# First rows of a hybrid SSD and MLP layer: shift and scale of tiles 1 to 5 singly, products high by high first

## The chip, the core and the metric

The kernel runs on one core of a Trainium2 chip. The metric is the time of one execution on the device, in microseconds (us). TensorE, VectorE (DVE), ScalarE (ACT), GpSimd (POOL) and the DMA queue of SyncE (SP) are the engines that appear in the rows; PEld is TensorE's weight load, which overlaps its products.

## The reference

The layer takes 256 latent tokens x and 256 context tokens ctx of width 2048, normalises each row, scales and shifts it by values that a vector c (for ctx: c_ctx) gives through a matrix w_ada, and projects the result with w_in. Cut to what the change touches:

```python
shift, scale, gate = jnp.split(silu(c) @ w_ada + b_ada, 3, axis=-1)
shift_c, scale_c, gate_c = jnp.split(silu(c_ctx) @ w_ada + b_ada, 3, axis=-1)
hc = _rmsnorm(ctx, g_pre) * (1.0 + scale_c) + shift_c
hx = _rmsnorm(x, g_pre) * (1.0 + scale[:, None]) + shift[:, None]
zc = hc @ w_in[:, :XBC_W + DT_W]
zx = hx @ w_in
```

What follows (convolution, a scan in both directions, a gated MLP, two norms, the output projection and the residual with gate) is the same before and after.

## The kernel before, in words

The model width is cut into 16 tiles (KT) of 128 rows. The token axis has 512 columns: the context half CTX is columns 0 to 255, the latent half 256 to 511. x stands transposed in `xT`.

All large products are done in three: a value is split into a high part (rounded to fp32r) and a low part (the rest), and high by high, high by low and low by high are added up in PSUM (`mm3`, lines 141 to 143). For the normalised rows the parts are `hhi` and `hlo`, for the weights `hi_st` and `lo_st`.

The **first rows** are the stage before the large weight stream. It makes `hhi` and `hlo` for all 16 tiles and, as each tile is ready, adds its share to the dt product (`psdt`, 512 columns, two products a tile: lines 418) and to seven output tiles psx0 to psx6. psx3 and psx6 have only the 256 latent columns. So a tile's products are 17 of 512 columns and 6 of 256.

Shift and scale of a tile need a product of silu(c) and silu(c_ctx) (`sc`, 32 columns, two used) with two megabytes of w_ada, the ada loads 2n and 2n+1. They run on 32-column groups of TensorE, four side by side. There are three forms:
- tile 0: `ada_mm` (line 249), 64 products of 64 columns, each of four column groups holding 32 of the tile's rows; `ada_fin` (line 257) transposes the result from PSUM on DVE, and two ACT operations (lines 262, 264) make `ha` (scale) and `hb` (shift);
- tiles 1 to 3: `ada_rows` (line 219), 16 products of 256 columns, each column group holding a quarter of the sum; `ada_keep` (224) copies that to SBUF, `ada_sum` (230) adds the four groups up and turns them with two products, `ada_one` (235, 237) makes `ha` and `hb` from PSUM;
- tiles 4 to 15 in pairs: `ada_mm` with 128 columns for two tiles at once, four ada loads, then `ada_fin` and `ada_ab`.

`make_h` (lines 365, 368, 370) then multiplies both halves of x by scale and 1/rms (`rb`) on DVE, adds the shift on ACT (that is `hhi`) and makes `hlo` on DVE. `split_hi` (ACT, line 352), `split_dt` (DVE, 356) and `split_lo` (DVE, 360) split the weights, `wst`.

The order on TensorE, DVE, ACT and POOL is written out by hand. For each tile kt, `row_steps(kt)` gives a list: ("m", -1) to ("m", 6) are the products dt and psx0 to psx6 of tile kt, the other letters prepare tile n = kt + 1. `STEPS` names their functions. SP's loads are issued in program order: for each kt the ada loads 2kt+6 and 2kt+7 and the weights of tile kt+2. ada loads have six buffers, weights three, the parts of the weights three. `warm` issues products with no use while the kernel waits for its first data.

After the first rows the weights w_xbc, w_lat and w_out stream through in pieces of 1 MB.

Of the kernel before, what the change touches and what calls it, by code (L numbers as in the profile page):

```python
# [8 lines left out]
F32 = mybir.dt.float32  # L9
F32R = mybir.dt.float32r  # L10
BF16 = mybir.dt.bfloat16
AF = mybir.ActivationFunctionType
ALU = mybir.AluOpType
PSUM = bass.MemoryType.PSUM

P = 128
D = 2048
# [8 lines left out]
WST = 64 + NST * P  # L26

WH = 64 + 3 * P
NSING = 4

LAST = (-1, 4, 5, 0, 1, 2, 3, 6)

# [12 lines left out]
def tile_hybrid_ssd_mlp(  # L45
# [126 lines left out]
    def spt(shape, name):  # L172
        return sps.tile(shape, F32, tag="s", name=name)
# [33 lines left out]

    ada_ps = {}

    def ada_rows(c):  # L210

        u, k0 = c // 2, 8 * (c % 2)
        if k0 == 0:
            ada_ps[u] = spt([P, 512], f"psada{u}")
        ps = ada_ps[u]
        raw = ada_raw.pop(c)
        for kk in range(8):
            g = kk % 4
            nc.tensor.matmul(ps[32 * g : 32 * g + 32, 0:256], lhsT=sc[:, k0 + kk, :], rhs=raw[:, kk * 256 : (kk + 1) * 256],
                             start=k0 == 0 and kk < 4, stop=k0 > 0 and kk >= 4)  # L220

    def ada_keep(u):
        cp = st2.tile([P, 256], F32, tag="cp", name=f"adac{u}")
        nc.vector.tensor_copy(cp, ada_ps[u][:, 0:256])
        ada_ps[u] = cp, ada_ps[u][:, 256:260]

    def ada_sum(u):
        cp, pt = ada_ps[u]
        for q in range(2):
            nc.tensor.matmul(pt[:, 2 * q : 2 * q + 2], lhsT=cp[:, q * P : (q + 1) * P], rhs=sel[:, 0, 0:2],  # L230
                             start=True, stop=True)

    def ada_one(u):
        pt = ada_ps.pop(u)[1]
        nc.scalar.activation(ha[:, u, :], pt[:, 0:2], AF.Identity, bias=bsc1[:, u : u + 1],
                             scale=pc[:, C_GPRE + u : C_GPRE + u + 1])
        nc.scalar.activation(hb[:, u, :], pt[:, 2:4], AF.Identity, bias=pc[:, C_BADA + u : C_BADA + u + 1])

    def ada_mm(ci):
        u, n, k0, nk = ada_place(ci)  # L240
        if k0 == 0:
# [10 lines left out]
    def ada_fin(u):  # L252

        ps = ada_ps.pop(u)
        n = 64 * len(UNITS[u])
        ada_ps[u] = tr = st2.tile([P, 128], F32, tag="row", name=f"adat{u}")
        nc.vector.transpose(tr[:, 0:n], ps[:, 0:n])
        ada_ab(u, 0)

    def ada_ab(u, q):  # L260
        kt, tr = UNITS[u][q], ada_ps[u]
        nc.scalar.activation(ha[:, kt, :], tr[:, 64 * q : 64 * q + 2], AF.Identity, bias=bsc1[:, kt : kt + 1],
                             scale=pc[:, C_GPRE + kt : C_GPRE + kt + 1])
        nc.scalar.activation(hb[:, kt, :], tr[:, 64 * q + 32 : 64 * q + 34], AF.Identity,
                             bias=pc[:, C_BADA + kt : C_BADA + kt + 1])
# [6 lines left out]

    def wst_load(kt):
        w = st3.tile([P, WST], F32, tag="wst", name=f"wst{kt}")
        nc.sync.dma_start(w, wst[kt])
        wraw[kt] = w

    for t in range(4):
# [24 lines left out]
    def warm(*ns):  # L303
        for n in ns:
            nc.tensor.matmul(psw[:, 0:n], lhsT=ones, rhs=ones[:, 0:1].to_broadcast([P, n]), start=True, stop=True)
# [25 lines left out]
    nc.vector.reciprocal(rc, rc)  # L331
    nc.vector.tensor_copy(ss4.rearrange("p (b i) -> p b i", i=32), bc(rc, 2, 32))
    nc.vector.transpose(rb, ss4)
    ada_mm(0)
    ada_mm(1)
    warm(512, 512)
    psdt = spt([P, TOK], "psdt")
    psx = []
    for i in range(6):
# [18 lines left out]
    def split_lo(kt, a=64, b=WST):  # L358
        hi, lo = sp0[kt]
        nc.vector.tensor_tensor(lo[:, a - 64 : b - 64], wraw[kt][:, a:b], hi[:, 64 + a : 64 + b].bitcast(F32), op=ALU.subtract)  # L360

    def make_h(kt):
        sl = (slice(256, 512), slice(0, 256))
# [17 lines left out]
    def row_steps(kt):  # L381


        m = [("m", i) for i in range(-1, NST)]
        if kt == KT - 1:
            out_ = [("m", i) for i in LAST]
            out_.insert(3, ("t", 0))
            for i in range(2):
                out_.insert(out_.index(("m", 4 + i)) + 1, ("z", i))
            return out_  # L390
        n = kt + 1
        s_ = [("c", n), ("d", n), ("l", n)]

        a = [("a", c) for c in range(2 * kt + 2, min(2 * kt + 6, 2 * KT))] if n >= NSING and kt % 2 else []
        f = [("f", (n - NSING) // 2 + NSING)] if kt % 2 else []
        f2 = [("f2", (n - NSING) // 2 + NSING)] if kt % 2 else []
        c_, d_, l_, h_ = s_ + [("h", n)]
        if n < NSING:
            r = [("r", 2 * n), ("r", 2 * n + 1)]
            g = m[4:5] + [("g", n), ("o", n), h_]  # L400
            if n < 3:
                q = 5 - n
                return m[:q] + r + [c_, ("k", n), d_, ("l1", n)] + g + [("l2", n)] + m[q:4] + m[5:]
            return m[:3] + r + s_ + [("k", n)] + g + m[3:4] + m[5:]
        if n == NSING:
            return m[:2] + a[:2] + m[2:3] + a[2:] + [c_] + f + [d_, ("l1", n), h_, ("l2", n)] + f2 + m[3:]
        if n == NSING + 1:
            return m[:3] + [h_] + s_ + m[3:]
        if n == NSING + 2:
            return m[:2] + a + s_ + f + [h_] + f2 + m[2:]  # L410
        return s_ + a + f + [h_] + f2 + m

    STEPS = {"a": ada_mm, "f": ada_fin, "f2": lambda u: ada_ab(u, 1), "r": ada_rows, "k": ada_keep, "g": ada_sum, "o": ada_one,
             "h": make_h, "c": split_hi, "d": split_dt, "l": split_lo,
             "l1": lambda n: split_lo(n, 64, WH), "l2": lambda n: split_lo(n, WH)}

    def dt_mm(kt, low):
# [26 lines left out]
    split_hi(0, 0, WH)  # L444
    ada_fin(0)
    split_dt(0)
    make_h(0)
    split_lo(0, 64, WH)
    split_hi(0, WH)
    split_lo(0, WH)  # L450
    for kt in range(KT):
# [810 lines left out]
def _layout(i):  # L1262
    import numpy as np

    i = {k: np.asarray(v) for k, v in i.items()}
    x, c, cx = i["x"][0], i["c"][0], i["ctx"][0]
    w_in, w_out, w_ada = i["w_in"][0], i["w_out"][0], i["w_ada"][0]
    order = _tile_order()
    a = {}
    xc = np.concatenate([cx, x], axis=0)  # L1270
    a["xch"] = xc.T.reshape(4, 4, P, TOK).transpose(0, 2, 1, 3).reshape(4, P, D)
    a["xtok"] = x.reshape(2, P, D)
    a["ccols"] = np.stack([c.reshape(KT, P).T, i["c_ctx"].reshape(KT, P).T], axis=2)
    wada = np.empty((48, P, D), w_ada.dtype)
    ss = w_ada[:, : 2 * D].reshape(KT, P, 2, KT, 4, 32)[:, :, ::-1].transpose(0, 1, 4, 3, 2, 5)
    for kt in range(NSING):
        r = ss[:, :, :, kt] if kt == 0 else ss[:, :, :, kt].transpose(0, 1, 3, 2, 4)
        wada[2 * kt : 2 * kt + 2] = r.reshape(2, 8, P, 256).transpose(0, 2, 1, 3).reshape(2, P, D)
    for m in range(NSING, KT, 2):
        wada[2 * m : 2 * m + 4] = ss[:, :, :, m : m + 2].reshape(4, 4, P, 512).transpose(0, 2, 1, 3).reshape(4, P, D)  # L1280
    wada[32:] = w_ada[:, 2 * D :].reshape(KT, P, 16, P).transpose(2, 3, 0, 1).reshape(16, P, D)
    a["wada"] = wada
    cw = i["conv_w"][0].reshape(5, 32, P)[:, order].transpose(2, 1, 0).reshape(P, 160)
    cb = i["conv_b"][0].reshape(32, P)[order].T
    a["pcols"] = np.concatenate(
        [i["b_ada"][0].reshape(48, P).T, i["g_pre"][0].reshape(KT, P).T, i["g_ssd"][0].reshape(KT, P).T,
         i["g_mlp"][0].reshape(KT, P).T, i["b_s"][0].T, cw, cb], axis=1)
    a["dtp"] = np.stack([i["dt_bias"][0].reshape(64), i["a_log"][0].reshape(64)])
    a["dskip"] = i["d_skip"].reshape(1, 32)
    a["gpost"] = i["g_post"].reshape(1, D)  # L1290
    a["gv"] = i["g_v"].reshape(1, D)
    a["crow"] = c.reshape(1, D)
    wk = w_in.reshape(KT, P, -1)
    xbc = wk[:, :, :4096].reshape(KT, P, 32, P)[:, :, order]
    a["wst"] = np.concatenate([wk[:, :, 4096:4160], xbc[:, :, list(FIRST)].reshape(KT, P, NST * P)], axis=2)
    a["wxbc"] = xbc[:, :, list(REST)].transpose(2, 1, 0, 3).reshape(len(REST), P, D)
    cols = {"z": 4160, "u": 6208, "v": 8256, "m": 10304}
    blocks = []
    for n in "vumz":
# [29 lines left out]
```

## Time and profile before

| | us |
|---|---|
| median of 3 runs | 989.73 |
| lowest and highest run | 989.63, 991.26 |
| span of the profiled execution, first to last instruction | 987.9 |
| TensorE busy in the span | 978.8 |
| DVE busy | 621.4 |
| ACT busy | 495.4 |

A row of the timeline has the start in us, the duration in us (for a row that merges several instructions, from the first's start to the last's end), the engine, the line of the kernel, the operation, output <- inputs, the tile's shape and, in brackets, the idle time of the engine just before it with what ended it. Records of consecutive products overlap, so the distance of two starts is what a product costs, and not its duration. On TensorE each fp32 product stands as two records, each fp32r product as one.

### The profile page before, as it was taken

What the parts mean: (1) busy time and instruction counts of PE and PEld (TensorE: products, weight loads), DVE (VectorE), ACT (ScalarE), POOL (GpSimd) and SP (SyncE); (2) the same over time, 40 slices, a digit from 0 to 9 for tenths busy, and PEclk for the clock granted to TensorE, in tenths of its full rate; (3) what the DMA queues carried; (4) which work ended last, traced back from release to release, by engine and by line L of the source; (5) the groups of instructions that cost most, each with busy time, mean ns of one, the idle gap of its engine ahead of it and who ended that gap; (6) DMA issues with size and microseconds to landing.
All of it is one profiled execution on the core that took longest, in us unless ns stands there. A gap on an engine that the chain in (4) does not pass through costs nothing.

```text
span 987.9 us, 13929 instructions
## 1 busy us (share of the span) xinstructions
PE 978.8 (99%) x5502; PEld 792.6 (80%) x5502; DVE 621.4 (63%) x949; ACT 495.4 (50%) x762; POOL 112.5 (11%) x162
## 2 busy tenths in 40 slices
PE   9999999999999999999999999999999999999997
PEld 4688888778887878787888888887888888888885
DVE  4444488868886566756767766767555564445636
ACT  4233358566665554545445343454565563346522
POOL 0000002432453222224000000000000000000000
PEclk9999999999999999999999999999999999999999
DMA  9999844233323424145877768774455446556722
GB/s 372 421 418 418 352 149 166 86 129 128 128 75 139 142 98 145 43 169 206 297 302 284 275 257 296 280 274 170 170 180 203 171 170 213 178 206 228 282 86 85
DMA packets 31985, 207.26 MB, mean 210 GB/s; under 512 B 4128, under 2 KB 4384, under 8 KB 8496
## 3 DMA queue, kind: packets, MB, share of 16 engines
q1 hardware_dynamic: 29232, 192.79, 52.0%
q0 software_dynamic: 2112, 12.65, 3.7%
q8 instruction: 43, 0.70, 0.3%
q10 hardware_dynamic: 576, 0.94, 0.3%
q14 instruction: 22, 0.18, 0.1%
HBM read 204.20 MB, written 2.16 MB: 209 GB/s over the span
## 4 chain that ended last, share of the span: by engine, by line
PE 92%; DMA 4%; ACT 2%; DVE 1%; SPq 0%; issue 0%; ACTq 0%
PE pa L1108 12%; PE pa L1110 12%; PE pa L1109 12%; PE psx L141 9%; PE psx L143 9%; PE psx L142 9%; PE pm L1157 3%; PE pm L1155 3%; PE pm L1156 3%; DMA wst<-in_wst_dram 3%; PE pq L1157 2%; PE pq L1156 2%; PE pq L1155 2%; PE psada L249 2%; PE psc L778 1%; PE pso L831 1%
## 5 line engine op out<-in xcount | busy, mean ns | idle before, releaser
L85 DVE TENSOR_TENSOR lo_w<-w,hi_w 128x1024 fp32r<-128x1024 f32 x173 | 210.7, 1224 | 146.0 <-ACT hi_w L84 145.9
L84 ACT CAST hi_w<-w 128x1024 fp32r<-128x1024 f32 x173 | 182.1, 1053 | 204.5 <-PE pa L1110 129.4
L1108 PE MATMUL pa<-hi_w,hhi 128*128 128x512 f32 x512 | 202.3, 395 | 0.0
L1110 PE MATMUL pa<-hi_w,hlo 128*128 128x512 f32 x512 | 199.5, 390 | 0.0
L1109 PE MATMUL pa<-lo_w,hhi 128*128 128x512 f32 x512 | 199.3, 389 | 0.0
L141 PE MATMUL psx<-hhi,hi_w 128*128 128x512 f32 (+1 forms) x400 | 153.4, 383 | 0.0
L143 PE MATMUL psx<-hhi,lo_w 128*128 128x512 f32 (+1 forms) x400 | 145.9, 365 | 0.0
L142 PE MATMUL psx<-hlo,hi_w 128*128 128x512 f32 (+1 forms) x400 | 145.7, 364 | 0.0
L1108 PEld LDWEIGHTS pa<-hi_w,hhi 128*128 128x128 f32 x512 | 96.2, 188 | 20.5 <-issue 1.6
L1110 PEld LDWEIGHTS pa<-hi_w,hlo 128*128 128x128 f32 x512 | 96.1, 188 | 20.3
L1109 PEld LDWEIGHTS pa<-lo_w,hhi 128*128 128x128 f32 x512 | 96.2, 188 | 19.5 <-issue 0.2
L576 DVE SCALAR_TENSOR_TENSOR xbc<-psx,pc,xbc 128x248 f32<-128x248 f32 (+1 forms) x204 | 83.6, 473 | 34.8 <-ACT xbc L560 33.9
L501 DVE TENSOR_TENSOR lo_w<-w,hi_w 128x1024 fp32r<-128x1024 f32 x61 | 77.1, 1271 | 23.7 <-ACT hi_w L495 23.6
L141 PEld LDWEIGHTS psx<-hhi,hi_w 128*128 128x128 f32 x400 | 75.5, 189 | 13.4 <-issue 2.9
L143 PEld LDWEIGHTS psx<-hhi,lo_w 128*128 128x128 f32 x400 | 75.4, 188 | 12.5
L142 PEld LDWEIGHTS psx<-hlo,hi_w 128*128 128x128 f32 x400 | 75.6, 189 | 12.2 <-issue 1.7
L495 ACT CAST hi_w<-w 128x1024 fp32r<-128x1024 f32 x61 | 63.5, 1044 | 26.0 <-PE psx L142 12.9
L966 DVE SCALAR_TENSOR_TENSOR junk<-gate,cb 128x2048 bf16<-128x2048 f32 x16 | 36.7, 2291 | 24.1 <-DMA gate<-in_wada_dram 24.1
L1155 PE MATMUL pm<-hi_w,hhi 128*128 128x512 f32 x128 | 50.0, 390 | 0.0
L1156 PE MATMUL pm<-lo_w,hhi 128*128 128x512 f32 x128 | 49.9, 390 | 0.0
L1157 PE MATMUL pm<-hi_w,hlo 128*128 128x512 f32 x128 | 49.7, 389 | 0.0
L730 ACT ACTIVATE R<-R,y 128x128 f32<-128x128 f32 x128 | 38.8, 391 | 0.0
(248 smaller groups left out, 1333.6 us busy)
## 6 DMA issues: line engine op xcount, KB each, us to landing
w<-in_wlat_dram SPq DMA_DIRECT2D x64, 1024.0 KB, 4.8
w<-in_wout_dram SPq DMA_DIRECT2D x32, 1024.0 KB, 4.8
ada<-in_wada_dram SPq DMA_DIRECT2D x30, 1024.0 KB, 13.4
w<-in_wxbc_dram SPq DMA_DIRECT2D x25, 1024.0 KB, 4.8
gate<-in_wada_dram SPq DMA_DIRECT2D x16, 1024.0 KB, 5.5
R<-acs POOLq DMA_DIRECT2D x8, 1024.0 KB, 5.2
wst<-in_wst_dram SPq DMA_DIRECT2D x15, 480.0 KB, 14.0
xT<-in_xch_dram SPq DMA_DIRECT2D x4, 1024.0 KB, 8.0
```

The lines of the kernel that those rows point to most:

```text
L84: nc.scalar.copy(hi, raw)
L85: nc.vector.tensor_tensor(lo, raw, hi.bitcast(F32), op=ALU.subtract)
L141: nc.tensor.matmul(ps, lhsT=whi, rhs=hhi[k][:, s], start=start, stop=False)
L142: nc.tensor.matmul(ps, lhsT=whi, rhs=hlo[k][:, s], start=False, stop=False)
L143: nc.tensor.matmul(ps, lhsT=wlo, rhs=hhi[k][:, s], start=False, stop=stop)
L576: nc.vector.scalar_tensor_tensor(ao, zi, cw[:, k : k + 1], ao, op0=ALU.mult, op1=ALU.add)
L1108: nc.tensor.matmul(pa[tk], lhsT=hhi[k][:, t], rhs=whi[:, w], start=k == 0, stop=False)
L1109: nc.tensor.matmul(pa[tk], lhsT=hhi[k][:, t], rhs=wlo[:, w], start=False, stop=False)
L1110: nc.tensor.matmul(pa[tk], lhsT=hlo[k][:, t], rhs=whi[:, w], start=False, stop=k == KT - 1)
L1155: nc.tensor.matmul(p, lhsT=yh[:, t], rhs=whi[:, w], start=j == 0, stop=False)
L1156: nc.tensor.matmul(p, lhsT=yh[:, t], rhs=wlo[:, w], start=False, stop=False)
L1157: nc.tensor.matmul(p, lhsT=yl[:, t], rhs=whi[:, w], start=False, stop=hf == 0 and j == 15)
```

## The change

- `NSING` goes from 4 to 6: tiles 0 to 5 have shift and scale made singly, tiles 6 to 15 in pairs.
- `ada_rows`, `ada_keep`, `ada_sum` and `ada_one` are gone. All single tiles take `ada_mm` and `ada_fin`, with w_ada laid out for it. For them `ha` is made on DVE and `hb` on ACT.
- The latent half of x is multiplied by 1/rms ahead of time (`scale_x`). `make_h1` makes the latent half of `hhi` with one ACT operation that has scale and shift, the context half as before. `make_l1` makes `hlo`, its latent half with two DVE operations.
- `first_tiles` issues dt and psx0 to psx2 of tiles 0 to 5 together: four products high by high, three with the weights' low part, four with the rows' low part; for tile 0 the high by high ones in two halves, latent first.
- The step lists of tiles 0 to 5 are rewritten. psx3 and psx4 stand ahead of the ada products (for tile 0: psx4 ahead, psx3 between the two), psx5 and psx6 behind the preparation of the next tile. The lists for n = NSING, NSING + 1 and NSING + 2 move by two tiles; in the first of them the ada products now stand ahead of psx3.
- The weights of single tiles are loaded in two pieces (448 and 512 columns); the weights of tiles 4 and 5 are now issued ahead of ada loads 10, 11 and 12, 13.
- The second `warm` call has 256 columns less.

```diff
-NSING = 4
+NSING = 6
     def ada_fin(u):
...
         nc.vector.transpose(tr[:, 0:n], ps[:, 0:n])
-        ada_ab(u, 0)
+        if u < NSING:
+            nc.vector.tensor_scalar(ha[:, u, :], tr[:, 0:2], pc[:, C_GPRE + u : C_GPRE + u + 1], bsc1[:, u : u + 1],
+                                    op0=ALU.mult, op1=ALU.add)
+            nc.scalar.activation(hb[:, u, :], tr[:, 32:34], AF.Identity, bias=pc[:, C_BADA + u : C_BADA + u + 1])
+        else:
+            ada_ab(u, 0)
...
-        nc.sync.dma_start(w, wst[kt])
+        for a, b in ((0, WH), (WH, WST)) if kt < NSING else ((0, WST),):
+            nc.sync.dma_start(w[:, a:b], wst[kt][:, a:b])
...
+    LAT, CTX = slice(256, 512), slice(0, 256)
+
+    def scale_x(kt):
+        nc.vector.tensor_tensor(xT[:, kt, LAT], xT[:, kt, LAT], rb[:, LAT], op=ALU.mult)
+
+    scale_x(0)
     ada_mm(0)
     ada_mm(1)
-    warm(512, 512)
+    warm(512, 256)
...
+    def make_h1(kt):
+        xl, xc = xT[:, kt, LAT], xT[:, kt, CTX]
+        al, ac = ha[:, kt, 0:1], ha[:, kt, 1:2]
+        bl, bc_ = hb[:, kt, 0:1], hb[:, kt, 1:2]
+        nc.scalar.activation(hhi[kt][:, LAT], xl, AF.Identity, bias=bl, scale=al)
+        nc.vector.scalar_tensor_tensor(xc, xc, ac, rb[:, CTX], op0=ALU.mult, op1=ALU.mult)
+        nc.scalar.activation(hhi[kt][:, CTX], xc, AF.Identity, bias=bc_)
+
+    def make_l1(kt):
+        xl, xc = xT[:, kt, LAT], xT[:, kt, CTX]
+        full = yseg(2 + kt % 2)[:, LAT]
+        nc.vector.tensor_scalar(full, xl, ha[:, kt, 0:1], hb[:, kt, 0:1], op0=ALU.mult, op1=ALU.add)
+        nc.vector.tensor_tensor(hlo[kt][:, LAT], full, hhi[kt][:, LAT].bitcast(F32), op=ALU.subtract)
+        nc.vector.scalar_tensor_tensor(hlo[kt][:, CTX], xc, hb[:, kt, 1:2], hhi[kt][:, CTX].bitcast(F32),
+                                       op0=ALU.add, op1=ALU.subtract)
...
+        tail_ = [("d", n), ("h1", n), ("l1", n), ("hl", n), ("c2", n), ("l2", n)]
+        if n == 1:
+            return [("o", 0), ("x", 1), m[5], ("a", 2), m[4], ("a", 3), ("c1", 1), ("f", 1)] + tail_ + m[6:]
         if n < NSING:
-            r = [("r", 2 * n), ("r", 2 * n + 1)]
-            g = m[4:5] + [("g", n), ("o", n), h_]
-            if n < 3:
-                q = 5 - n
-                return m[:q] + r + [c_, ("k", n), d_, ("l1", n)] + g + [("l2", n)] + m[q:4] + m[5:]
-            return m[:3] + r + s_ + [("k", n)] + g + m[3:4] + m[5:]
+            return [("o", kt), ("x", n)] + m[4:6] + [("a", 2 * n), ("a", 2 * n + 1), ("c1", n), ("f", n)] + tail_ + m[6:]
         if n == NSING:
-            return m[:2] + a[:2] + m[2:3] + a[2:] + [c_] + f + [d_, ("l1", n), h_, ("l2", n)] + f2 + m[3:]
+            return [("o", kt)] + a + [c_] + f + [d_, ("l1", n), h_, ("l2", n)] + f2 + m[4:]
...
+    def first_tiles(kt):
+        whi, wlo = sp0[kt]
+        w = [whi[:, i * P : (i + 1) * P] for i in range(4)]
+        for v, s in enumerate((LAT, CTX) if kt == 0 else (slice(0, 512),)):
+            for i, ps in enumerate((psdt, psx[0], psx[1], psx[2])):
+                nc.tensor.matmul(ps[:, s], lhsT=w[i], rhs=hhi[kt][:, s], start=kt == 0 and v == 0, stop=False)
+        for i in range(3):
+            nc.tensor.matmul(psx[i], lhsT=wlo[:, i * P : (i + 1) * P], rhs=hhi[kt], start=False, stop=False)
+        for i, ps in enumerate((psdt, psx[0], psx[1], psx[2])):
+            nc.tensor.matmul(ps, lhsT=w[i], rhs=hlo[kt], start=False, stop=False)
```

## Rows read from the trace of the kernel before

**Rows 1.** Busy us by stretch: PE, PEld, DVE, ACT, POOL, clock, DMA share, GB/s

```profile
22.00:126.00 104.00, 103.06 (x1225) 83.86 (x1226) 48.58 (x106) 36.80 (x77) 0.00 (x0) 1.00 0.98 403
...
126.00:987.00 861.00, 855.34 (x4090) 700.24 (x4088) 562.18 (x820) 448.70 (x668) 110.10 (x147) 1.00 0.50 183
```

**Rows 2.** The same columns, stretches of 4 us

```profile
4.00:8.00 4.00, 4.00 (x14) 1.34 (x12) 1.80 (x5) 3.17 (x6) 0.00 (x0) 1.00 1.00 418
...
16.00:20.00 4.00, 3.96 (x137) 2.77 (x134) 2.36 (x5) 0.75 (x2) 0.00 (x0) 1.00 1.05 395
...
20.00:24.00 4.00, 3.35 (x10) 1.54 (x9) 3.06 (x7) 2.03 (x6) 0.00 (x0) 1.00 1.00 408
...
108.00:112.00 4.00, 4.00 (x22) 3.33 (x20) 2.52 (x6) 1.91 (x3) 0.00 (x0) 1.00 0.97 400
```

**Rows 3.** Timeline, TensorE: first products of tiles, tile 2's ada products

```profile
22.00 0.50 PE L418 MATMUL psdt<-hhi,hi_st 128*128 128x512 f32 x1 [0.39 <-ACT hhi L368]
...
30.81 0.50 PE L418 MATMUL psdt<-hhi,hi_st 128*128 128x512 f32 x1 [0.63 <-ACT hhi L368]
...
32.84 1.93 PE L219 MATMUL psada<-ada,sc 128*32 128x256 f32 x32
...
45.71 0.40 PE L418 MATMUL psdt<-hhi,hi_st 128*128 128x512 f32 x1
...
54.54 0.40 PE L418 MATMUL psdt<-hhi,hi_st 128*128 128x512 f32 x1
...
59.17 0.40 PE L418 MATMUL psdt<-hhi,hi_st 128*128 128x512 f32 x1
...
68.00 0.50 PE L418 MATMUL psdt<-hhi,hi_st 128*128 128x512 f32 x1
...
81.20 0.40 PE L418 MATMUL psdt<-hhi,hi_st 128*128 128x512 f32 x1
```

**Rows 4.** Chain of waits: start us, us, what

```profile
49.41 14.03 DMA wst<-in_wst_dram
```

**Rows 5.** Timeline, ACT: casts of tiles 1, 6, 8; hhi of 8

```profile
27.64 0.99 ACT L352 CAST hi_st<-wst 128x960 fp32r<-128x960 f32 x1 [5.18 <-DMA wst<-in_wst_dram]
...
63.52 0.99 ACT L352 CAST hi_st<-wst 128x960 fp32r<-128x960 f32 x1 [5.15 <-PE psada L249]
...
76.12 1.00 ACT L352 CAST hi_st<-wst 128x960 fp32r<-128x960 f32 x1 [2.74 <-DMA wst<-in_wst_dram]
...
79.64 0.91 ACT L368 ACTIVATE hhi<-xT,hb 128x256 fp32r<-128x256 f32 x2 [0.43 <-DVE xT L365]
```

**Rows 6.** Timeline of all engines: tile 0's chain

```profile
17.44 1.39 PEld L249 LDWEIGHTS psada<-ada,sc 128*32 128x32 f32 x96
...
19.03 0.49 PEld L249 LDWEIGHTS psada<-ada,sc 128*32 128x32 f32 x32 [0.21 <-DMA ada<-in_wada_dram]
...
19.53 0.56 ACT L352 CAST hi_st<-wst 128x448 fp32r<-128x448 f32 x1 [1.71 <-DMA wst<-in_wst_dram]
...
19.61 1.99 PE L305 MATMUL psw<-ones 128*128 128x512 f32 x4
...
19.75 0.25 DVE L257 STREAM_TRANSPOSE adat<-psada 128x64 f32<-128x64 f32 x1 [0.37 <-PE psada L249]
...
20.04 0.39 ACT L262 ACTIVATE ha<-adat,bsc,pc 128x2 f32<-128x2 f32 x1
...
20.12 0.23 DVE L356 TENSOR_TENSOR hi_st<-wst,hi_st 128x64 fp32r<-128x64 f32 x1
...
20.46 0.88 DVE L365 SCALAR_TENSOR_TENSOR xT<-xT,ha,y 128x256 f32<-128x256 f32 x2
...
21.04 0.91 ACT L368 ACTIVATE hhi<-xT,hb 128x256 fp32r<-128x256 f32 x2 [0.43 <-DVE xT L365]
```

**Rows 7.** Groups of 16 to 130 us: busy us, mean ns, idle before

```profile
L230 PE MATMUL psada<-sel,adac 128*128 128x2 f32 x12 | 1.8, 256 | 0.0
```

**Rows 8.** Timeline, weight loads: second half of ada 3

```profile
26.55 0.16 PEld L219 LDWEIGHTS psada<-ada,sc 128*32 128x32 f32 x8 [0.27 <-DMA ada<-in_wada_dram]
```

More of the change, by code (lines that the diff above doesn't have):

```diff
@@ L208, in tile_hybrid_ssd_mlp @@
     ada_ps = {}
[L210 to L237, printed above, removed]
     def ada_mm(ci):
@@ L288, in tile_hybrid_ssd_mlp @@
     ada_load2(1)
-    wraw[0] = st3.tile([P, WST], F32, tag="wst", name="wst0")
-    for a, b in ((0, WH), (WH, WST)):
-        nc.sync.dma_start(wraw[0][:, a:b], wst[0][:, a:b])
+    wst_load(0)
     ada_load(2)
@@ L411, in row_steps @@
         return s_ + a + f + [h_] + f2 + m
-    STEPS = {"a": ada_mm, "f": ada_fin, "f2": lambda u: ada_ab(u, 1), "r": ada_rows, "k": ada_keep, "g": ada_sum, "o": ada_one,
-             "h": make_h, "c": split_hi, "d": split_dt, "l": split_lo,
+    def first_tiles(kt):
[8 more added lines that the diff above has]
+            nc.tensor.matmul(ps, lhsT=w[i], rhs=hlo[kt], start=False, stop=False)
+    STEPS = {"a": ada_mm, "f": ada_fin, "f2": lambda u: ada_ab(u, 1), "o": first_tiles, "x": scale_x, "h1": make_h1,
+             "hl": make_l1, "c1": lambda n: split_hi(n, 0, WH), "c2": lambda n: split_hi(n, WH), "h": make_h, "c": split_hi, "d": split_dt, "l": split_lo,
              "l1": lambda n: split_lo(n, 64, WH), "l2": lambda n: split_lo(n, WH)}
@@ L446, in tile_hybrid_ssd_mlp @@
     split_dt(0)
-    make_h(0)
+    make_h1(0)
     split_lo(0, 64, WH)
+    make_l1(0)
     split_hi(0, WH)
@@ L1276, in _layout @@
     for kt in range(NSING):
-        r = ss[:, :, :, kt] if kt == 0 else ss[:, :, :, kt].transpose(0, 1, 3, 2, 4)
-        wada[2 * kt : 2 * kt + 2] = r.reshape(2, 8, P, 256).transpose(0, 2, 1, 3).reshape(2, P, D)
+        wada[2 * kt : 2 * kt + 2] = ss[:, :, :, kt].reshape(2, 8, P, 256).transpose(0, 2, 1, 3).reshape(2, P, D)
     for m in range(NSING, KT, 2):
```

## The prediction

> **What bounds the kernel now.** I read the busy times by stretch first, with the stage that the change touches apart from the rest: from 22 to 126 us TensorE is busy 103.06 of 104 us and DMA 0.98 of the time; from 126 us on TensorE is just as full, 855.34 of 861, but DMA is at 0.50 [rows 1]. So two things are full at once there, and nothing of the stage but its length reaches the rest, which TensorE bounds. The stretches of 4 us make it sharper: from 4:8 to 108:112, all 27, the DMA share is 0.97 or more [rows 2]. Last I read TensorE's rows in order of time, for the start of each tile's products (its first dt product, line 418): 22.00, 30.81, ... 45.71, 54.54, 59.17, 68.00, ... 81.20 [rows 3]. An idle time stands at two of them: 0.39 us at tile 0 and 0.63 us at tile 1.
>
> The chain of waits says what ends last there: from 49.41 to 63.4 us it runs through the load of tile 6's weights [rows 4], and tile 6's cast starts as it lands, at 63.52; TensorE starts tile 6 4.5 us later [rows 5, 3]. The casts date the loads: tile 1 at 27.64, tile 6 at 63.52 [rows 5]. Between them lie 12 ada loads of 1.049 MB and five weight tiles of 0.492 MB, 15.04 MB in 35.88 us: 0.419 MB per us, so 6.18 us for one tile's 2.59 MB.
>
> **Prices.** From 54.54 to 59.17 TensorE does one tile's products and nothing else [rows 3]: 17 of 512 and 6 of 256 columns, worth 20 of 512, in 4.63 us, 0.2315 each. The new first block (11) is then 2.55 us, psx3 with psx4 1.04, psx5 with psx6 1.04. A change from these to the ada products costs about 0.1 us on the way in and the same on the way out (tile 0's ada weights end at 19.52, the next TensorE work starts at 19.61) [rows 6].
>
> **Edit 1: the ada products of tiles 1 to 3 in column groups.** 16 products of 256 columns become 64 of 64. Tile 2's, in the old form, start at 32.84 and last 1.93 us [rows 3]. Tile 0 has the new form already: 17.44 to 19.52 less a DMA wait of 0.21, 1.87 us; its first 96 weight loads took 1.39 us, 14.5 ns each [rows 6]. So no difference. The Trainium skill has a rule against such splitting (TensorE: Matmul & The Clock Gate, "Wait — 56ns, not 53.3ns?"): matmul starts never come closer than about 25 ns, however few the columns. By that rule the 128 records of a tile would take an estimated 3.2 us; the trace does not agree.
>
> **Edit 2: the summation products go** (lines 224, 230, 235). 12 records, 1.8 us in all, 0.6 us a tile for three tiles [rows 7], all on TensorE's path. DVE's copy ahead of them goes too, beside other work.
>
> **Edit 3: the new chain from the last ada product to the first product.** Old, at tile 0 [rows 6]: product end to transposition 0.14; 0.29 to ha on ACT; 0.42 to the first x operation; 0.58 to hhi; 0.91 for both halves; 0.05 to TensorE at 22.00: 2.39 us. New: 0.14; transposition 0.25; ha on DVE; the 64-column subtraction 0.15; x of the context half 0.58 to hhi; one half of the pair about 0.49; 0.05. The latent half needs only ha and hb and is done before that. ha on DVE is in no row: nothing at best, the transposition's 0.25 at worst (64 columns against 2); I take 0.2. Sum 1.86, bounds 1.66 and, if nothing of it helps, 2.39. Its cover on TensorE is psx5 and psx6, 1.04 and 0.1, so TensorE idles 0.72 us a tile (0.5 to 1.25). In the old order of tiles 2 and 3 more products lay there and no idle time stands before 45.71 [rows 3]. So edit 2's 0.6 is spent again.
>
> The scaling of the latent half by x/rms ahead (half of "xT" 0.88 x2, 0.44 us) is placed where DVE sat idle 0.37 us before the transposition [rows 6], and for later tiles in the tile's own slack: nothing, or 0.07 at tile 0. Shorter warming takes 0.5 us from a stretch that ended in idle time; the clock stayed at 1.00 through both idle times [rows 1].
>
> **Edit 4: tile 0 high by high first.** hhi of the latent half at about 20.9 (hb waits for the 0.56 us cast begun at 19.53), TensorE free of warming at 21.0, latent half to 21.46; the context half is ready then; high by high ends at 21.95, high weight-low at 22.65, low at 23.57. Low parts wait for nothing: the split ends at 21.3 and hlo at 22.3. Then psx4 24.26, ada 2 to 25.3, psx3 25.75; ada 3 is not free to end: its second half lands at 26.55 [rows 8], so 27.1. With 1.86 behind it tile 1 starts at 29.0; if the first piece of tile 1's weights lands only with the rest at 27.64 [rows 5], 0.56 of cast and 1.27 of chain give 29.5. I take 29.2, against 30.81.
>
> **Edit 5: tiles 4 and 5 singly.** A single step is now 2.55 + 1.04 + 0.1 + 1.87 + 1.86 = 7.42. Old: 7.45 for one of tiles 1 and 2 (30.81 to 45.71), but 13.46 for tiles 3 and 4 (45.71 to 59.17), whose pair of ada units went through in one go [rows 3]. Two steps of 7.42 are 14.84, 1.4 us more. So: tile 2 at 36.6, tile 3 44.0, tile 4 51.5, tile 5 58.9. Loads are in time: weights of tiles 2 to 5, now sent ahead of the ada loads of two tiles on, land at 33.8, 40.0, 46.2, 52.4 by 6.18 us each, and ada work ends at 34.7, 42.2, 49.6, 57.0. The ada loads 10 to 13 behind them on SP's queue land about 1.2 us later, and are read 5 us later than now. The five extra issues on SP hide in the 14 us from issue to landing [rows 4]; ada 16 and 17 wait for buffers until about 57, while loads up to 63.5 are queued.
>
> Tile 6: 58.9 + 2.55 + 0.1 + 3.63 (four ada chunks) = 65.2; the chain of a pair is 2.39 and 0.06 for 128 columns and 0.2 for the weight split now ahead of x: 67.8, against 68.00. **Sum: 0.2 us earlier.** Next is tile 8: its cast at 76.12 is a landing, and hhi ends at 79.64 + 0.91 = 80.55 whatever TensorE does [rows 5], while TensorE came at 81.20 [rows 3]. That is the ceiling: 0.6 us, unless loads land earlier. From there every step keeps its order, so 0.2 us reaches the end: span 987.7. The median of the three runs lies 1.8 us above the span of the profiled execution, so 989.5.
>
> **Rivals.**
> Uncovered chain, slower: if the five waits stay at tile 0's old 2.39 us, TensorE idles 1.25 a tile. It decides from 1.91 us on (0.2 us spread over four steps). Tile 1 then starts at 29.5, steps take 7.95, tile 6 starts at 70.2: 2.2 us late, 991.9. For it: ha's price is in no row, and DVE takes the subtraction ahead of x. Against: two ACT steps leave the path. 0.13.
> Split loads, slower: the five halved weight loads slow a full DMA stream. In the stretches where tile 0's two pieces moved, 395 and 408 GB/s stand against 418 in the first [rows 2]: 0.32 us at most, 1.6 for five; tile 8's ceiling moves to 82.2, 1.0 us late: 990.7. Against: the share stayed full, so other bytes moved. 0.10.
> The start wins more, faster: chain at 1.66, tile 1 at 28.8: tile 6 at 66.6, 1.4 early, cut to the ceiling's 0.6: 989.1. With loads 1 us earlier, which fewer bytes in flight could give, 988.3. For it: tile 1's first weight piece is smaller. 0.14.
> Issue-bound ada products, slower: if 64 columns cost starts and not columns, tile 0's 2.08 us with its wait bounds it: 0.21 more for each of five tiles, 990.6. The 14.5 ns speak against it. 0.03. By the skill's 25 ns it would be an estimated 1.3 us a tile, 6 in all.
>
> **How the numbers follow.** The forecast, 989.5 with 988.9 to 990.4 of its own, has 0.60. About 0.2% (2.0 us) is what a measurement of this kernel can tell from no change. The range goes to 988.2 below, the third rival's far end, and to 991.4 above, short of the first rival's end; it leaves out some 0.15. Faster by over 0.2%, under 987.75, needs more than the ceiling: 0.04. Slower, over 991.7: half of the first rival, most of the last, and ends of others: 0.11. Within: 0.85.
>
> **What would show it.** In the changed profile: tile 1's first product at 29.2 (right if 28.9 to 29.6); idle TensorE of 0.7 us before each of tiles 2 to 5; tile 4 at 51.5, ahead of 54.54, and tile 5 at 58.9, all but level with 59.17; tile 8's products right behind its hhi at 80.6 to 81.1. Wrong: idle times over 1.2 us, ada products over 2.1 us a tile, or tile 8's cast away from 76.1, which would say that the loads moved.

## The result, and the profile after

The changed kernel is slower by 0.39%: median 994.15 us of 5 runs (992.84 to 994.82) against 990.06 us (989.63 to 991.26), ratio 1.0039 with a 95% interval of 1.0027 to 1.0052. The prediction was 989.5 us with a range that ended at 991.4. The profiled execution of after took 993.53 us, its span 991.5 us, against 987.9 before.

The page of after, its first lines and the fetch queue of the instructions (packets, MB, share of 16 DMA engines):

```profile
span 991.5 us, 14777 instructions
## 1 busy us (share of the span) xinstructions
PE 979.0 (99%) x5910; PEld 795.8 (80%) x5910; DVE 623.7 (63%) x965; ACT 494.8 (50%) x761; POOL 112.5 (11%) x162
...
q8 instruction: 46, 0.75, 0.3%
```

The same two lines of before:

```profile
PE 978.8 (99%) x5502; PEld 792.6 (80%) x5502; DVE 621.4 (63%) x949; ACT 495.4 (50%) x762; POOL 112.5 (11%) x162
...
q8 instruction: 43, 0.70, 0.3%
```

TensorE's busy time is as before, so nearly all of the 3.6 us by which the span grew is idle time. But an equal busy time is not equal work: the summation's 1.8 us [rows 7] are gone, and products at a lower clock, shown below, took some 1.5 us more. What grew is the number of TensorE's instructions: 5502 records of products and as many of weight loads before, 408 more of each now, 816 together; each record is an instruction, two to an fp32 product. The queue that brings instructions moved 43 packets (0.70 MB) before and 46 now, 16 KB each: 11004 records to 43 packets and 11820 to 46 make some 256 to a packet.

The timeline of TensorE in after shows where the time went (rows 3 are its rows of before; columns as there):

```profile
28.96 0.50 PE L413 MATMUL psdt<-hhi,hi_st 128*128 128x512 f32 x1 [0.55 <-ACT hhi L349]
...
32.70 1.88 PE L220 MATMUL psada<-ada,sc 128*32 128x64 f32 x118
36.96 0.58 PE L220 MATMUL psada<-ada,sc 128*32 128x64 f32 x10 [2.38 <-issue]
37.47 0.80 PE L141 MATMUL psx<-hhi,hi_st 128*128 128x512 f32 x1
...
39.56 0.63 PE L413 MATMUL psdt<-hhi,hi_st 128*128 128x512 f32 x1
...
43.64 1.99 PE L220 MATMUL psada<-ada,sc 128*32 128x64 f32 x128
45.56 0.50 PE L141 MATMUL psx<-hhi,hi_st 128*128 128x512 f32 x1
...
47.42 0.50 PE L413 MATMUL psdt<-hhi,hi_st 128*128 128x512 f32 x1 [0.54 <-ACT hhi L349]
...
54.99 0.50 PE L413 MATMUL psdt<-hhi,hi_st 128*128 128x512 f32 x1 [0.54 <-ACT hhi L349]
...
62.57 0.50 PE L413 MATMUL psdt<-hhi,hi_st 128*128 128x512 f32 x1 [0.54 <-ACT hhi L349]
...
71.42 0.50 PE L424 MATMUL psdt<-hhi,hi_st 128*128 128x512 f32 x1
```

Tile 1 starts at 28.96, tiles 3 to 5 follow each other at 7.57 us. But tile 2 starts 10.6 us after tile 1. In the middle of tile 2's ada products, after 118 of 128, TensorE stands still for 2.38 us, and what ended that is "issue": no data, no other engine, nothing that the profile shows. The products behind it run slow: 0.43 us from one to the next at 38.06 and 38.49, where 0.23 is usual. The busy times by stretch say why (columns as in rows 1; the clock is the third from the right):

```profile
32.00:36.00 4.00, 2.57 (x122) 2.01 (x120) 0.00 (x0) 0.57 (x1) 0.00 (x0) 1.00 1.01 419
36.00:40.00 4.00, 3.04 (x18) 2.49 (x19) 2.28 (x8) 2.05 (x5) 0.00 (x0) 0.63 1.02 418
40.00:44.00 4.00, 4.00 (x42) 3.13 (x44) 1.33 (x3) 0.22 (x1) 0.00 (x0) 0.94 1.00 402
```

The granted clock is 0.63 and then 0.94: the lower of its two levels, 1.2 GHz, for part of these stretches, right behind the standstill.

**The theory** (S in the expectations, for supply): TensorE ran out of instructions. They come in pieces of 256, the next piece is sent for only about when the one before it is entered, and the new ada form uses up a piece faster than the next one arrives. The rival is that the new form or the new order is dear by itself, wherever it stands: in its products, its chain, its loads or the clock.

### The profile page after: what moved, and what is told of

The parts are those of the page before. It is cut to its first block, busy times and chain, and to the rows that moved or that the text cites. A ratio compares the mean times of both kernels' runs of the same rounds, so it can differ in the third digit from the quotient of the medians.

```text
span 991.5 us, 14777 instructions
## 1 busy us (share of the span) xinstructions
PE 979.0 (99%) x5910; PEld 795.8 (80%) x5910; DVE 623.7 (63%) x965; ACT 494.8 (50%) x761; POOL 112.5 (11%) x162
## 4 chain that ended last, share of the span: by engine, by line
PE 94%; ACT 2%; DMA 1%; DVE 1%; issue 1%; SPq 0%; ACTq 0%
PE pa L1115 12%; PE pa L1117 12%; PE pa L1116 12%; PE psx L141 9%; PE psx L143 9%; PE psx L142 9%; PE psada L220 3%; PE pm L1162 3%; PE pm L1164 3%; PE pm L1163 3%; PE pq L1164 2%; PE pq L1162 2%; PE pq L1163 2%; DMA ada<-in_wada_dram 1%; PE psc L785 1%; PE pso L838 1%
```

## The experiments

### The column groups alone

The kernel before, with tiles 1 to 3 in column groups and nothing else of the change: no summation, old order, old loads.

```diff
-            r = [("r", 2 * n), ("r", 2 * n + 1)]
-            g = m[4:5] + [("g", n), ("o", n), h_]
+            r = [("a", 2 * n), ("a", 2 * n + 1)]
+            g = m[4:5] + [h_]
...
-                return m[:q] + r + [c_, ("k", n), d_, ("l1", n)] + g + [("l2", n)] + m[q:4] + m[5:]
+                return m[:q] + r + [c_, ("f", n), d_, ("l1", n)] + g + [("l2", n)] + m[q:4] + m[5:]
...
-        r = ss[:, :, :, kt] if kt == 0 else ss[:, :, :, kt].transpose(0, 1, 3, 2, 4)
+        r = ss[:, :, :, kt]
```

> The kernel before with one part of the change: the ada products of tiles 1 to 3 in column groups (64 products of 64 columns, transposed from PSUM), without the summation; order, halves of x and tiles 4, 5 as before. Theory S (supply): TensorE ran out of instructions in tile 2's ada products, because each 256 instructions come as one 16 KB piece through DMA queues that are full, and the dense products use up 256 of them in 1.9 us. Then the gap stands here too, 1 to 2.5 us of idle put down to issue in or right behind the ada products of tile 2 or 3, with some us at the half clock behind it, and the time is 990.5 to 993. Rival O (order): the new order of work makes TensorE wait there for something that the trace doesn't show. Then there is no gap, and three summations of 0.6 us less give 988 to 989.8.

992.27 us, ratio 1.0019 (1.0009 to 1.0028). The waits of TensorE from 0 to 140 us (line, releaser: us in total, times, longest) have one row of "issue":

```profile
PE psx L141 <- issue: 2.4, 1, 2.4
```

It ends at 38.00 us, three products behind tile 2's ada products, and the granted clock is 0.75 and 0.82 in the two stretches from 36 us. So half of the loss needs neither the new chain nor the new order. And the gap has a place in the stream of instructions, not in the work. TensorE's products and weight loads from the start to the gap, in after and in this kernel (stretch; PE and PEld with their counts, then as in rows 1):

```profile
0.00:34.50 34.50, 32.77 (x478) 19.11 (x478) 16.43 (x40) 13.00 (x24) 2.37 (x15) 1.00 0.96 384
```

```profile
0.00:37.99 37.99, 32.45 (x478) 17.70 (x478) 18.04 (x43) 15.20 (x29) 2.39 (x15) 1.00 0.96 388
```

478 and 478 in both, though one gap lies inside tile 2's ada products and the other behind them.

### When the piece came

The DMA records of after date the fetch. From 30.65 us on, where TensorE entered the piece that ran out, no packet of the instruction queue moves for 3.8 us; the first starts at 34.45 us. The view of DMA queues from 30.65 to 34.40 and from 34.40 to 35.60:

```profile
q1 hardware_dynamic: 436, 1.59, 103.7%
```

```profile
q1 hardware_dynamic: 67, 0.49, 100.5%
q8 instruction: 1, 0.02, 5.5%
```

TensorE goes on at 36.96 us, 2.5 us after the fetch starts (2.45 in the kernel with the column groups alone). Wait and fetch make 6.3 us, while the piece, with 236 of its 256 instructions in tile 2's ada products, was used up in 3.9 us; the difference is the gap. The old kernel's pieces last longer: its fetches up to 76 us start at 30.33, 43.89, 53.56, 65.17 and 75.21 us, 10 to 14 us apart; those of after at 28.20, 34.45, 40.47, 48.08, 55.36, 61.50 and 69.58.

The same delay shows in all 14 traces. With TensorE's semaphore and drain instructions counted too, which the views above leave out, both gaps stand behind exactly 961 instructions. Counted so, the first packet of the queue belongs to the piece that begins behind 449 instructions, the next to the one behind 705, and so on by 256 to the end of each of the 14 traces; of these 617 pieces none is entered less than 2.26 us after its packet starts, and at the eight gaps put down to "issue" up to 140 us it is 2.26 to 2.51 us. What does not hold is that the entry into a piece itself sends for the next. From 10 to 112 us, where the DMA share around the fetch is over 0.9, 105 of 140 fetches start 2 to 4 us behind the edge (the entry into the piece before the one they bring), but the others range from 1.6 us ahead of it to 6.0 behind; and past 150 us, where DMA is at about half, the median fetch starts 2.9 us ahead. What does send for a piece is not shown.

The Trainium skill describes this (Runtime: NRT & Kernel Launch, "Instruction fetch mechanics"): instructions come in blocks of 16 KiB, 256 each, and the next is fetched while the present one runs. The trace agrees, 16 KB and 256. The Trainium skill adds there that the cost of crossing a boundary is "mostly hidden"; here it was 2.38 us and a lowered clock.

### The same stream at another place: the gap is not the form's

The column groups alone again, with useless early products cut finer: 112 instructions more before the first tile, no work more.

```diff
-    warm(512, 512, 512, 512)
+    warm(*[128] * 15, 64, 64)
...
-            warm(512)
-            if k < 12:
-                warm(256)
+            warm(*([128] * 6 if k < 12 else [256] * 2))
...
-    warm(512, 512)
+    warm(256, 256, 256, 256)
```

> groups_alone with 112 more instructions ahead of 17 us in the same way. Theory S: shortest piece 6.2 us, so no gap or one under 0.4 us, clock 1.00, and what the loads allow: 989.2 to 990.3 (992.27 without the shift). Rival O: the gap stays, 991.5 to 992.5.

989.88 us, ratio 0.9998 (0.9988 to 1.0008). The ada products are the same, the ends of the pieces fall elsewhere, every piece lasts at least 4.9 us up to 70 us, and all that TensorE waits for from 0 to 140 us is

```profile
PE psdt L416 <- ACT hhi L366: 1.4, 4, 0.4
PE psw L305 <- DVE ones L110: 1.1, 1, 1.1
PE psada L249 <- DMA ada<-in_wada_dram: 1.0, 2, 0.7
PE psx L434 <- DVE lo_st L358: 0.3, 1, 0.3
```

No issue. 2.4 us went with nothing but a shift of the stream: this is the plainest evidence for the theory. The control, the kernel before with 108 instructions more, and an earlier one with 40 (`warm(*[128] * 12, 256, 256)`):

> The kernel before with 108 more instructions ahead of 17 us and nothing of the change. Two pieces now fall into the paired ada products: 4.6 to 5.2 us near 60.6 and 3.9 us near 98.8. In before_shift such a piece near 73 us lasted 3.75 us without a gap, because its successor's fetch began 0.4 us after the edge and not 3 us. If the fetch waits 3 us or more here, as behind most edges: a gap of 1 to 2.5 us near 102 or 65 and 990.8 to 993. If an edge at the start of paired ada products always sees its fetch begin early: no gap, 989.7 to 990.6.

> The kernel before with its first useless products cut finer (12 of 128 columns and 2 of 256 for 4 of 512): 40 instructions of TensorE more in the first 7 us, at about the same TensorE time; nothing of the change. Theory S says that what counts is how long TensorE takes over one piece of 256 instructions (edges at record 961 and every 256 before and behind it): in the kernel before the shortest takes 7.1 us and no gap stands; shifted by 40, one piece lies whole in the paired ada products near 72.5 us and takes 3.7 us. So a gap of 2 to 3 us put down to issue near 76 us, perhaps a half clock behind it, and 991.5 to 994.5. Rival O: the order and the forms of the products are what they were, so no gap and 990.1, as before.

989.69 us (0.9999, 0.999 to 1.0009) and 989.71 us (0.9996, 0.9987 to 1.0005), no gap in either. For the second I had expected one near 76 us, where a piece lasts only 3.75 us; it didn't come, because the fetch of that piece's successor started 0.44 us after the edge and not some 3 us. In the first, a piece of 3.63 us at 99.09 saw the fetch start at the edge. So the wait ahead of a fetch varies, and a short piece alone makes no gap.

The changed kernel itself, shifted by 72 instructions:

```diff
-    warm(512, 512, 512, 512)
+    warm(*[128] * 15, 64, 64)
...
-            warm(512)
-            if k < 12:
-                warm(256)
+            warm(*([128] * 4 + [256] if k < 4 else [512, 256] if k < 12 else [256] * 2))
...
-    warm(512, 256)
+    warm(256, 256, 256)
```

> The changed kernel, whole, with 72 instructions of TensorE more ahead of 17 us (useless products cut finer), nothing else. Theory S: the piece that ran out in tile 2 now lasts 6.5 us, so no gap there and no half clock behind it; the shortest pieces last 4.6 to 4.9 us, near 55, 60 and 97 us, so there may be a gap of up to 1.5 us if their fetch waits 3 us or more. Tile 3's first product at 44.2 to 45 instead of 47.42, tile 6's at 68.2 to 70, 990.2 to 992. Rival O (the new order or forms cost the 4 us by themselves): 993.5 to 994.5 as before the shift.

995.07 us, ratio 1.0049 (1.003 to 1.0067): the expected gain missed. But the gaps moved. TensorE's timeline:

```profile
21.41 0.38 PE L280 MATMUL psw<-ones 128*128 128x256 f32 x1 [0.30 <-issue]
...
29.91 0.54 PE L220 MATMUL psada<-ada,sc 128*32 128x64 f32 x23 [2.52 <-issue]
...
43.62 1.99 PE L220 MATMUL psada<-ada,sc 128*32 128x64 f32 x128
...
69.69 0.42 PE L220 MATMUL psada<-ada,sc 128*32 128x128 f32 x6 [0.74 <-issue]
```

Tile 2's gap is gone, and one stands in tile 1's ada products. Counted as above, 447, 701 and 2232 products and loads lie ahead of these three, and after's 956 come one piece behind 701. With the semaphore and drain instructions it is 449, 705 and 2241, and 961 in after: in order, one, one and five times exactly 256 apart. The fetch of the piece that came at 29.91 started at 27.43, 6.0 us after the edge at 21.41: the longest wait of all. The clock stays at 1.00 here, and tile 6 starts at 72.51, against 71.42 in after.

Sixteen useless products of 16 columns ahead of tile 2's first ada product, in the changed kernel:

```diff
+        if ci == 4:
+            for _ in range(16):
+                nc.tensor.matmul(ps[:, 256:272], lhsT=ones, rhs=ones[:, 0:1].to_broadcast([P, 16]), start=True, stop=True)
```

> The changed kernel with 16 useless products of 16 columns (64 instructions more) right ahead of tile 2's ada products. Theory S: the gap is tied to a place in the instruction stream, so it comes 64 instructions earlier: after about 86 of the 128 records of tile 2's ada products instead of 118, and lasts 2.4 to 3.2 us. Rival O or a late load of tile 2: it stays after 118 records. Time 993 to 995.5 in both.

997.98 us in a single execution, and missed: the gap did not come earlier, it went. The added products took 4.36 us for 32 records, from 32.75 on. The granted clock fell while they still ran, with no idle time before it: 0.93 from 32 to 36 us and 0.50 from 36 to 40, and tile 2's ada products behind them took 3.57 us instead of 1.92. In this time the piece came. In their place stands a gap of 1.00 us at 72.60, behind 2233 products and loads: the same edge as the third one above.

### Emptier queues: the change without its gap

The changed kernel with an eighth of the bytes of ada loads 4 to 31; instructions, order and places of the edges stay. It leaves out seven eighths of w_ada for tiles 2 to 15, so it does not compute the layer.

```diff
-        nc.sync.dma_start(raw, src)
+        nc.sync.dma_start(raw[:, 0:n], src[:, 0:n])
...
-            ada_raw[ci] = load_raw(wada[ci], f"ada_{ci}")
+            ada_raw[ci] = load_raw(wada[ci], f"ada_{ci}", 256 if ci >= 4 else 2048)
...
-                o = (kk * 4 + g) * n
+                o = (kk * 4 + g) * n % (256 if ci >= 4 else 2048)
```

> The changed kernel with an eighth of the bytes of the ada loads 4 to 31 (256 columns loaded and used eight times, so shift and scale of tiles 2 to 15 are not the reference's). Instructions of TensorE and their edges as in the changed kernel. Theory S with full queues as the reason that a piece comes late: DMA share under 0.5 from 28 us on, the piece's fetch begins 1 to 3 us earlier than 34.45, the gap is under 0.5 us, tile 6's first product at 66.5 to 67.5, and 986.5 to 988. If fetching is slow by itself: the gap stays at 1.5 to 2.4 us.

990.46 us in a single execution, span 988.4: the gap went, as expected, but the time that I had expected with it, 986.5 to 988, did not come. DMA is at 0.48 and 0.34 in the stretches where after had 1.01 and 1.02:

```profile
32.00:36.00 4.00, 4.00 (x139) 3.21 (x137) 1.11 (x5) 0.77 (x2) 0.00 (x0) 1.00 0.48 153
36.00:40.00 4.00, 3.46 (x17) 2.90 (x17) 2.51 (x6) 1.50 (x4) 0.00 (x0) 1.00 0.34 90
```

The view of DMA queues from 31.40 to 32.45 us has the fetch:

```profile
q1 hardware_dynamic: 94, 0.15, 62.3%
q8 instruction: 1, 0.02, 5.7%
```

It starts at 31.46, 0.7 us after the piece before it was entered at 30.75, against 3.8 us. That piece is used up in 3.69 us, about as fast as in after, and there is no gap. So with full queues the fetch starts late, and with emptier ones in time; that the full queues are the cause rests on this pair of runs. At the next four edges the wait was 1.8, 0.7, 0.7 and 0.6 us, and in after 3.5, 3.1, 3.2 and 2.1. What sets the single wait when the queues are equally full stays open.

The run also shows what the change does to the first rows when nothing stalls. TensorE's timeline:

```profile
29.03 0.50 PE L413 MATMUL psdt<-hhi,hi_st 128*128 128x512 f32 x1 [0.55 <-ACT hhi L349]
...
32.80 1.99 PE L220 MATMUL psada<-ada,sc 128*32 128x64 f32 x128
...
36.58 0.50 PE L413 MATMUL psdt<-hhi,hi_st 128*128 128x512 f32 x1 [0.54 <-ACT hhi L349]
...
40.36 1.99 PE L220 MATMUL psada<-ada,sc 128*32 128x64 f32 x128
...
44.15 0.50 PE L413 MATMUL psdt<-hhi,hi_st 128*128 128x512 f32 x1 [0.54 <-ACT hhi L349]
...
51.71 0.50 PE L413 MATMUL psdt<-hhi,hi_st 128*128 128x512 f32 x1 [0.54 <-ACT hhi L349]
...
59.28 0.50 PE L413 MATMUL psdt<-hhi,hi_st 128*128 128x512 f32 x1 [0.54 <-ACT hhi L349]
...
68.12 0.50 PE L424 MATMUL psdt<-hhi,hi_st 128*128 128x512 f32 x1
```

Tile 3 starts at 44.15, in after at 47.42: 3.27 us. From the start of tile 2's ada products to that of tile 3's after takes 10.94 us (32.70 to 43.64) and this kernel 7.56 (32.80 to 40.36), 3.38 more. 2.38 of it is the gap; the gap also covers the 0.54 us of idle time ahead of tile 2; so 1.54 is left for the lowered clock. Tile 6 carries it on (71.42 against 68.12), and the span ends 3.1 us later.

Half the bytes, by the same edit with 1024 for 256, was meant as the same test:

```diff
...
-            ada_raw[ci] = load_raw(wada[ci], f"ada_{ci}")
+            ada_raw[ci] = load_raw(wada[ci], f"ada_{ci}", 1024 if ci >= 4 else 2048)
...
```

> The changed kernel with half of the bytes of the ada loads 4 to 31: only their first 1024 columns are loaded and used twice, so shift and scale of tiles 2 to 15 are not the reference's. Instructions of TensorE as in the changed kernel. Theory S with full queues as the cause: DMA share 0.6 to 0.7, no gap, the clock stays at 1.00, tile 6's first product at 66 to 67.5 instead of 71.42, time 987 to 989.5. If the supply of instructions is too slow by itself, whatever the loads do: the gap stays, time 993 or so.

It wasn't one: the queues stayed full up to 40 us. 992.06 us in a single execution, a gap of 1.48 us at 36.22 after the same 118 records, the fetch at 33.77 instead of 34.45. The clock stayed at 1.00 behind this shorter gap.

### Four tiles singly, and what binds without the gap

The changed kernel with `NSING = 4`, so that tiles 4 and 5 are a pair again:

```diff
-NSING = 6
+NSING = 4
```

> The changed kernel with tiles 4 and 5 in a pair again (NSING 4), the weights of tiles 4 and 5 in one piece. Theory S: the stream up to tile 2 is the same, so the gap stays (2.4 us, after 118 records) and the half clock behind it: 992 to 993.5. What a pair saves over two single tiles (1.1 to 1.4 us by the step lengths) shows at tile 6: its first product at 70.0 to 70.6 instead of 71.42. If the gap came from making six tiles singly, it is gone, and the time is 989 or less.

991.74 us, ratio 1.0015 (1.0005 to 1.0024). The gap is there, 2.07 us after 118 records, with the clock at 0.63 and 0.95 behind it; tile 6 starts at 69.47, earlier than the 70.0 to 70.6 that I had expected. The same kernel shifted by 108 instructions (the cut of the shift above, with `warm(256, 256, 256)` at its end), and then also with the weights' low part made behind x in the paired tiles:

```diff
-            return m[:2] + a + s_ + f + [h_] + f2 + m[2:]
-        return s_ + a + f + [h_] + f2 + m
+            return m[:2] + a + [c_] + f + [d_, h_, l_] + f2 + m[2:]
+        return a + [c_] + f + [d_, h_, l_] + f2 + m
```

> after_nsing4 with 108 more instructions ahead of 17 us, by cutting the useless products finer (same columns but for 0.2 us). Theory S: the edges move so that no piece is used up in under 6.2 us up to 112 us: no gap, or one under 0.4 us in tile 2 or 3, clock at 1.00, tile 6's first product at 65.5 to 67 (69.47 without the shift), and 988.7 to 990 by the ceiling that tile 8's weights set. Rival O: the gap stays in tile 2's ada products, 991.5 to 992.5.

> nsing4_shift, and for the paired tiles DVE transposes and makes x and hlo ahead of the large low part of the weights, so that hhi of tile 8 does not stand 4.4 us behind its cast. If the ceiling of the prediction is real, it goes up from 0.6 us to 2 us or more: tile 8's first product 0.5 to 1.5 us earlier than in nsing4_shift, and 987.8 to 989. If loads of ada or TensorE bound it instead: the same as nsing4_shift within 0.3 us.

990.13 us (1.0002, 0.9993 to 1.0011) and 989.74 us (1.0001, 0.9992 to 1.001): no gap, and no gain. In the first of them tiles 1 to 3 start at 29.90, 37.45 and 45.01, but tile 4 at 54.51 is level with rows 3's 54.54, and the timeline shows the load that holds it:

```profile
51.34 1.00 ACT L331 CAST hi_st<-wst 128x960 fp32r<-128x960 f32 x1 [5.87 <-DMA wst<-in_wst_dram]
```

```profile
54.51 0.50 PE L422 MATMUL psdt<-hhi,hi_st 128*128 128x512 f32 x1 [0.77 <-ACT hhi L363]
```

I had expected tile 6 at 65.5 to 67 us; it came at 68.09, 0.09 after that of before. Moving the weights' low part had tile 8's hhi ready 1.66 us earlier (78.99 instead of 80.65), yet tile 8 only from 81.29 to 81.02, and the whole time stays inside the interval. So in these kernels it is not the prediction's ceiling, tile 8's hhi, that holds tile 8.

### The order alone

`NSING = 4` with the old ada form, its summation products put back and everything else of the change kept:

```diff
...
-            return [("o", kt), ("x", n)] + m[4:6] + [("a", 2 * n), ("a", 2 * n + 1), ("c1", n), ("f", n)] + tail_ + m[6:]
+            return [("o", kt), ("x", n)] + m[4:6] + [("r", 2 * n), ("r", 2 * n + 1), ("c1", n), ("k", n), m[6], ("g", n), ("a1", n)] + tail_ + m[7:]
...
```

> The other half of the change alone: after_nsing4 with the old ada products for tiles 1 to 3 (16 of 256 columns, kept and summed), so the new order, tile 0 high by high first, half of x ahead, the halved weight loads and ha of tile 0 on DVE stay, and TensorE has about as many instructions as before. Theory S: no gap, clock 1.00; tile 1 at 29.5 to 30.3, idle times of 1 to 1.5 us ahead of tiles 2 and 3 since the summation lies in the chain, tile 4 at 54 to 55.5 by its loads, 989.3 to 990.8. Rival O: a gap like the changed kernel's and 992 to 994.

992.21 us, ratio 1.0026 (1.0016 to 1.0037), where no loss was expected, and no issue gap. Here the chain is too long: old form and new order leave 1.16 or 1.17 us of idle time ahead of each of tiles 1 to 3, for the data and not for instructions.

```profile
30.06 0.50 PE L442 MATMUL psdt<-hhi,hi_st 128*128 128x512 f32 x1 [1.16 <-ACT hhi L378]
30.39 0.86 PE L442 MATMUL psx<-hhi,hi_st 128*128 128x512 f32 x3
...
38.62 0.65 PE L442 MATMUL psdt<-hhi,hi_st 128*128 128x512 f32 x1 [1.17 <-ACT hhi L378]
39.07 1.48 PE L442 MATMUL psx<-hhi,hi_st 128*128 128x512 f32 x3
```

```profile
36.00:40.00 4.00, 2.83 (x14) 2.22 (x13) 2.86 (x8) 2.31 (x6) 0.00 (x0) 0.85 1.03 420
40.00:44.00 4.00, 4.00 (x17) 2.97 (x15) 0.56 (x2) 0.27 (x1) 0.00 (x0) 0.72 1.02 420
48.00:52.00 4.00, 3.21 (x8) 2.55 (x9) 2.29 (x6) 1.79 (x4) 0.00 (x0) 0.63 1.02 422
```

Behind the second and third of these idle times the granted clock falls, and the same three products take 1.48 us instead of 0.86; behind the first it doesn't. So the step from tile 2 to 3 (38.62 to 48.80) is 10.18 us and that from 1 to 2 is 8.56: 1.6 us for the clock, on top of 0.6 us more of idle time than in the new form. How often the clock falls differs between executions of this one kernel: the ten go from 991.1 us, with 0.999 granted over the whole span, to 995.98 with 0.994; the profiled one took 994.17 with 0.996, and those next to the median have 0.998 and 0.999. So the profile shows more of the clock's price than the median holds. I did not try the new order with that idle time filled.

## Why the prediction was wrong

**Edit 1 failed, and it alone decides.** "So no difference" priced the time of the 64-column products and not their number. The time was nearly right: a tile's ada products take 1.92 us (43.64 to 45.56), so the rival of issue-bound products falls. The Trainium skill's 25 ns as the least distance of two starts (TensorE: Matmul & The Clock Gate, "Wait — 56ns, not 53.3ns?") does not agree with the 15 ns a record here: in tile 3's, 6 or 7 ns lie between the four column groups and 35 or 36 to the next four. But 128 records of products and 128 of weight loads stand where 32 and 32 stood: 192 more a tile, a whole piece in 1.9 us. I looked at the queues that carry data and had the line of the instruction queue on the page; I did not ask how long its pieces last. No rival held this case, so the range was too narrow for it.

The part of the sum that failed, by its size: 2.38 of gap and 1.54 of lowered clock, less 0.54: 3.4 us priced at nothing. The statement "the clock stayed at 1.00 through both idle times" was about 0.39 and 0.63 us, and said nothing of longer ones; rows 1 begin where the first of them ends, so for it 20:24 of rows 2 has the 1.00.

**The other steps held**, by after and by the run with light loads (which cannot show whether full loads would have bound this kernel without its gap; no run shows that):
- Edit 2: without the summation the step of a tile in the old order is 6.86 and 6.80 us (30.83, 37.69 and 44.49 in the shifted kernel with column groups alone) against 7.45: 0.6 a tile, as priced.
- Edit 3: from the last ada product to the first product of the next tile 1.86 us (45.56 to 47.42), exactly the sum, and not by luck: from the transposition on the steps take 0.28, 0.20, 0.13, 0.57 and 0.49 us, each within 0.03 of its term; the idle time is 0.54, not 0.72, since the products that cover it take longer by that. The rival of the uncovered chain is refuted here; it is real in the order alone, at 1.17.
- Edit 4: tile 1 at 28.96, forecast 29.2. Its first piece of weights landed before the ada products ended: the cast starts at 27.03, in [rows 5] at 27.64.
- Edit 5: steps of 7.56, forecast 7.42, so tile 6 at 68.12 without the gap instead of 67.8. That is 0.12 later than before and not 0.2 earlier, and the span 988.4 instead of 987.7: no difference, as forecast, when the instructions come in time and the loads are light.
- The rival of split loads: tile 6's cast starts at 63.67 in after, with its landing as the releaser, 0.15 us later than in [rows 5]; the rival's five loads would make it 1.6. It falls.
- Loads bind too: with a shorter first part (four tiles singly, shifted) tile 4 waits for its weights. The third rival's earlier loads did not come.

Of the marks that I set, tile 1 and the idle times came out right; tile 4 at 54.99 instead of 51.5 and tile 5 at 62.57 instead of 58.9 came out wrong by the one gap (51.71 and 59.28 without it). Tile 8's cast is away from 76.12 too: its load landed at 78.87. That this is the gap as well, by buffers that came free later, is likely but not shown.

**What the change is worth.** Without the gap, four single tiles are level with before: 990.13 and 989.74 us. Six were seen without it only with light loads, level too. No kernel here beats the one before.

## What to carry to other kernels

When a product is split into many small ones, count instructions as well as columns: here TensorE ran dry beside full DMA queues in eight places, where a 256-instruction piece had been used up in 2.5 to 6.0 us. The gap is what is missing: the wait for the fetch, plus some 2.4 us from its start to the next instruction, less the time that the piece lasts. A short piece alone makes none (3.75 us, with a wait of 0.44), and a wait of 6.0 us made one behind a piece of 6.0. An idle time put down to "issue" that stays at the same count of instructions in different kernels is the sign; moving the stream by some dozens of instructions tells it from a cost of the work itself, though it is a test and no cure, since the edge may land in another dense stretch. And where the granted clock may fall behind an idle time of TensorE, price that too: here it cost 1.5 to 1.6 us more behind idle times of 1.2 to 2.4 us.

## What the runs showed of the hardware

- TensorE's instructions come in pieces of 16 KB and 256 instructions. Beside full queues 105 of 140 fetches start 2 to 4 us after the edge (1.6 ahead to 6.0 behind seen), with the ada loads cut to an eighth 0.6 to 1.8 us after it at the six edges from 30 to 63 us. No piece is entered less than 2.26 us after its fetch starts, and at the eight gaps it is 2.26 to 2.51 us.
- The granted clock fell to its lower level behind idle times of 2.38, 2.42 and 2.07 us (after, column groups alone, four tiles singly) and behind two of three of 1.17 us (order alone), and did not fall behind 2.52 (after shifted by 72), 1.48 (half the bytes) and 1.35 us (column groups alone, ahead of tile 1). It also fell with TensorE busy, during the products of 16 columns. What decides is not shown.
- Full-array products of 16 columns cost 0.136 us a record (4.36 us for 32), with part of them at the lower clock; products of 64 columns on the four column groups cost 15 ns a record (1.92 us for 128).
